# A gated three-mixer decoder block on one core: splits queued behind the gates' evictions, and another order inside the attention steps

## The chip, the cores and the metric

The kernel runs on one core of a Trainium2 chip. The metric is the device time of one execution in microseconds (us). The median of three runs of the kernel before is 353.12 us (352.27 to 354.44).

The core's engines each work through a queue of their own, in the order in which the program put the instructions there: TensorE (PE; its weight loads are shown as PEld), VectorE (DVE), ScalarE (ACT), GpSimd (POOL) and SyncE (SP), which issues the DMA transfers.

## What is computed

One decoder layer for 256 tokens of width 1024, in float32. The input is normed and multiplied by one wide weight matrix; from the product come queries, keys and values of three mixers, a gate for each mixer, and merge logits. The core of the reference:

```python
h = rmsnorm(x, norm_w[l])
proj = h @ w_in[l]
pieces = jnp.split(proj, IN_SPLIT_POINTS, axis=-1)
...
o_a = dilated_mixture(groups, slopes_a).reshape(B, S, D_A)
o_b = moba_attention(heads(b_q), heads(b_k), heads(b_v), slopes_b).reshape(B, S, D_B)
kv = rmsnorm(mem, mem_norm_w[l]) @ w_mem_kv[l]
m_k, m_v = jnp.split(kv, 2, axis=-1)
o_m = memory_cross_attention(heads(m_q), heads(m_k), heads(m_v)).reshape(B, S, D_M)
p_a = (o_a * jax.nn.silu(a_gate)) @ w_branch_a[l]
p_b = (o_b * jax.nn.silu(b_gate)) @ w_branch_b[l]
p_m = (o_m * jax.nn.silu(m_gate)) @ w_branch_m[l]
g_a, g_b, g_m = jnp.split(jax.nn.sigmoid(merge_logits + b_merge[l]), N_BRANCHES, axis=-1)
merged = g_a * p_a + g_b * p_b + g_m * p_m
x = x + merged @ w_out[l]
return rmsnorm(x, final_norm_w)
```

Mixer A has 8 heads in three dilation groups, mixer B 8 heads of causal attention, mixer M 4 heads over 256 memory tokens.

## The kernel before

**Chunks.** The weights are cut into 54 chunks (the list `PLAN`), nearly all of 1 MB. The main loop takes them in order: 0 to 5 are Bq, Bk and Bv, 6 to 10 the gates (b, b, a, a, m), 11 Mq, 12 Mk, 13 Mv, 14 to 31 mixer A, then merge logits and output products of the branches, and the last four the output projection. A full-precision product is made of three products in the faster format fp32r: the weights are split into a high part `wh` (ScalarE, line 93) and a low part `wl` (VectorE, line 94), and so are the activations (`hh`, `hl`). A chunk is two halves of 24 matmuls of 128x256: in each, 16 read `wh` (lines 232 and 233) and 8 read `wl` (line 235), in this order. There are three buffers for raw weights, three for `wh`, two for `wl`. So a part of chunk i can only be written when the chunk that held its buffer has been read.

**PSUM.** A chunk's result goes to one of three PSUM buffers (`pj`), which is free again when it has been evicted. The eviction of a gate is a tanh on ScalarE (line 645) and an operation of VectorE (line 647, tile `g`). Chunk 9 needs the buffer of chunk 6, chunk 10 that of chunk 7, and so on.

**Splits.** Queries and keys of mixer B are split too: `split_q` (lines 271 and 272) and `split_k` (283, 284 on ScalarE, 289, 290 on VectorE), for two halves of the heads (Bq0, Bk0, Bq1, Bk1). They are written out at chunks 6 to 11. The memory is normed by `mem_norm` (squares at line 171, then lines 143, 144, 175) and split by `mem_split` (line 218 on ScalarE, 219 on VectorE; tiles `mh`, `ml`), at chunks 9 to 11; chunk 12 reads them.

**Order.** On VectorE, ScalarE, GpSimd and SyncE a scheduler of the framework orders the instructions when the program is built: it places each by its own estimate of when the operands are ready, and so can place work well ahead of where it is written. `tc.issue_after(x)` keeps work behind instruction x. From chunk 8 on TensorE's order is as written.

**Attention steps.** The attention of each pair of heads is cut into steps, which `pump` slips between the halves of the chunks, two slots (one chunk) apart: for mixers B and M scores, transposes, products; for mixer A the first scores, transposes with the second scores, transposes, products. The steps of the next pair begin one chunk later (B, M) or two chunks later (A), so that several steps fall due in one slot. `chain` sorts them by slot and then by a second number: before, the later step of a pair goes first (`-j`). A step of scores needs two PSUM banks (pool `s`, two buffers), whose last readers are VectorE's minima (line 306), and a transpose needs rows that VectorE has scaled (line 314, tile `u`).

Of the kernel before, what the change touches and what calls it, by code (L numbers as in the profile page):

```python
# [1 line left out]

# [5 lines left out]
F32 = mybir.dt.float32  # L8
F32R = mybir.dt.float32r
BF16 = mybir.dt.bfloat16  # L10
AF = mybir.ActivationFunctionType
# [52 lines left out]
def kernel(ctx: ExitStack, tc: tile.TileContext, wts: bass.AP, xT_d: bass.AP, memT_d: bass.AP,  # L64
# [278 lines left out]
    def pair_steps_a(pair):  # L343
        hf, f = pair // 2, pair % 2
        us, pts, nbs = {}, {}, {}

        def view(n, g):
            return qkv["A" + n, hf, g].rearrange("p (f t) -> p f t", f=2)

        def scores(par):  # L350
            if par == 0:
                for s in range(2):
                    nbs[s] = tp.tile([P, 512], F32, tag="nb", name="nba")
                    nc.gpsimd.tensor_scalar(nbs[s], tab_a, SLOPES_A[2 * pair + s], 1.0, op0=ALU.mult, op1=ALU.mult)  # L354
            banks = [pa.tile([P, 512], F32, tag="s", name="sa") for _ in range(2)]
            for s in range(2):
                if par == 0:
                    out = banks[s].rearrange("p (a b) -> p a b", a=2)[:, :, 0:P]
                else:
                    out = banks[s][:, 0:S]  # L360
                score(out, qkv["Aq", hf, 0], qkv["Ak", hf, 0], s, f, slice(P * par, P * (par + 1)), slice(0, S))
            for g in range(1, 3):
                for s in range(2):
                    rows = slice(HD * s, HD * (s + 1))
                    for r in range(2):
                        ts = slice(P * par + 64 * r, P * par + 64 * (r + 1))
                        lo = P * (par + 1) + 64 * (g - 1)
                        nc.tensor.matmul(banks[s][64 * r:64 * (r + 1), lo:lo + 64], view("q", g)[rows, f, ts],
                                         view("k", g)[rows, f, ts], start=True, stop=True)
            for s in range(2):  # L370
                us[s, par] = tp.tile([P, 512], F32, tag="u", name="u", bufs=4)
                softmax(banks[s], nbs[s][:, P * (1 - par):P * (4 - par)], us[s, par], 0, 384)

        def trans(par):
            for s in range(2):
                if par == 0:
                    pts[s] = tp.tile([P, 3, 2, P], F32, tag="ptsb", name="ptsb", bufs=3)
                transposes(us[s, par], (0, 2, 1) if par == 0 else (0, 1, 2), pts[s][:, :, par, :])

        def pv():  # L380
            o = pa.tile([P, 512], F32, tag="o", name="oa", bufs=1)
            v0 = qkv["Av", hf, 0].rearrange("p (e c) -> p e c", e=2)
            vs = stacked[hf]
            for j in range(2):
                for s in range(2):
                    cols = slice(HD * (2 * f + s), HD * (2 * f + s + 1))
                    nc.tensor.matmul(o[HD * s:HD * (s + 1), 0:S], v0[:, j, cols],
                                     pts[s][:, j].rearrange("p e q -> p (e q)"), start=(j == 0), stop=False)
            for par in range(2):
                for r in range(2):  # L390
                    for s in range(2):
                        cols = slice(HD * (2 * f + s), HD * (2 * f + s + 1))
                        lo = P * par + 64 * r
                        nc.tensor.matmul(o[HD * s:HD * (s + 1), lo:lo + 64], vs[:, par, r, cols],
                                         pts[s][:, 2, par, 64 * r:64 * (r + 1)], start=False, stop=(par == 1 and r == 1))
            gated(o, "a", pair, False)

        return [lambda: scores(0), lambda: (trans(0), scores(1)), lambda: trans(1), pv]

    def pair_steps_b(pair):  # L400
        hf, f = pair // 2, pair % 2
# [68 lines left out]
    def chain(pairs, first, each):  # L470

        for n, fns in enumerate(pairs):
            for j, fn in enumerate(fns):
                steps.append((first + each * n + 2 * j, -j, fn))
        steps.sort(key=lambda z: z[:2])

    def out_mm(kc, wi, t):
# [46 lines left out]
                cs = slice(512 * (n // 2), 512 * (n // 2 + 1))  # L524
                nc.sync.dma_start(out[P * t:P * (t + 1), cs], yt[:, cs])

    late = []

    def evac_b(i, kind, key, ps, ps1):
        t = qkv[kind, key] = rtile(f"{kind}{key}")  # L530
# [15 lines left out]
    for i, (kind, key, src, col) in enumerate(PLAN):  # L546
# [15 lines left out]
        if i + 2 < NCH:  # L562
            for j in range(2 if i < 2 else 1):
                split(i + 2, j, 4 if i < 2 else 2)
        if i in (6, 8):
            hf = (i - 6) // 2
            qkv["Bqx", hf] = split_q(qkv["Bq", hf], 1.0, f"Bq{hf}")
        if i in (7, 11):
            hf = (i - 7) // 4
            qkv["Bkx", hf] = split_k(qkv["Bk", hf], f"Bk{hf}")  # L570
        if i == 9:
            mem_norm()
        if i in (10, 11):
            mem_split(4 * (i - 10), 4 * (i - 9))
        nat = kind[0] == "B"
        ah, al = (XH, XL) if nat else (HH, HL)
        if src == "mem":
# [64 lines left out]
                nc.scalar.mul(t, ps, -SCALE if kind == "Aq" else 1.0)  # L642
        elif kind == "G":
            th = tp.tile([P, 512], F32, tag="th", name="thg")
            nc.scalar.activation(th, ps, AF.Tanh, scale=0.5)
            g = gate[key] = rp.tile([P, 512], F32, tag="g", name=f"g{i}", bufs=5)
            nc.vector.scalar_tensor_tensor(g, th, 1.0, ps, op0=ALU.add, op1=ALU.mult)  # L647
        elif kind == "L":
            br, bk = key
            th = ths[br, bk] = tp.tile([P, 512], F32, tag="th", name="thl")  # L650
# [124 lines left out]
```

## Time and profile before

| | before |
|---|---|
| median of the runs | 353.12 us |
| profiled execution | 352.46 us |
| its span, first to last instruction | 350.6 us |
| TensorE busy | 337.4 us, 96% |
| VectorE busy | 232.5 us, 66% |
| ScalarE busy | 208.6 us, 60% |
| mean granted clock of TensorE | 0.989 |

The span is the time of the profiled execution without what lies around the program. Busy time says little on an engine that is always busy; what it waits for, and at which granted clock it works, is read from the views below. [...] All times in rows are microseconds from the start of the span, if not marked ns.

### The profile page before, as it was taken

How to read it: one execution, taken by the hardware profiler on the slowest of the kernel's cores; microseconds unless marked ns; L12 is line 12 of the kernel's file. 1: busy time of each engine (PE TensorE's matmuls, PEld its weight loads, DVE VectorE, ACT ScalarE, POOL GpSimd, SP SyncE). 2: the span in 40 equal slices, each digit the busy share in tenths (PEclk: the TensorE clock that was granted, in tenths of full speed). 3: DMA queues.
4: the chain of work that ended last, by engine and by line, in shares of the span. 5: the costliest groups of instructions: out<-in, count | busy, mean ns of one | idle time of the engine just before them, and what ended most of it. 6: DMA issues, size and time to landing. Idle time of an engine off the chain costs nothing.

```text
span 350.6 us, 7110 instructions
## 1 busy us (share of the span) xinstructions
PE 337.4 (96%) x2924; PEld 324.0 (92%) x2924; DVE 232.5 (66%) x402; ACT 208.6 (60%) x372; POOL 28.3 (8%) x40
## 2 busy tenths in 40 slices
PE   7999996999989999999999999999999999999992
PEld 4999995999989999899999999999999999999882
DVE  3859999658887457568756356866544748567554
ACT  6767899437776557766656365764643465546222
POOL 2501000000101000000101000010000214000022
PEclk9999998799999999999999999999999999999999
DMA  7997786646334463345333535444334366646003
GB/s 208 335 411 299 278 333 246 227 143 218 121 121 151 158 235 121 120 138 222 121 133 117 222 133 202 160 133 168 121 122 171 130 241 240 226 143 233 0 3 121
DMA packets 12945, 63.33 MB, mean 181 GB/s; under 512 B 1392, under 2 KB 2800, under 8 KB 6640
## 3 DMA queue, kind: packets, MB, share of 16 engines
q1 hardware_dynamic: 12912, 62.88, 49.9%
q8 instruction: 23, 0.38, 0.4%
q14 instruction: 10, 0.08, 0.1%
HBM read 61.82 MB, written 1.05 MB: 179 GB/s over the span
## 4 chain that ended last, share of the span: by engine, by line
PE 84%; DVE 6%; DMA 5%; ACT 2%; issue 1%; SPq 1%; POOL 0%; POOLq 0%; DVEq 0%
PE pj L232 16%; PE pj L235 16%; PE pj L233 16%; PE pj L252 4%; PE pj L254 4%; PE pj L253 4%; PE pt L320 3%; PE pw L232 3%; PE pw L233 3%; PE pw L235 3%; DMA wraw<-in_wts 3%; DMA xn<-in_x 2%; PE y L492 2%; PE y L491 2%; PE y L493 2%; DVE wl L94 2%
## 5 line engine op out<-in xcount | busy, mean ns | idle before, releaser
L94 DVE TENSOR_TENSOR wl<-wraw,wh 128x1024 fp32r<-128x1024 f32 (+2 forms) x117 | 129.4, 1143 | 60.1 <-issue 33.8
L93 ACT CAST wh<-wraw 128x1024 fp32r<-128x1024 f32 (+2 forms) x117 | 108.0, 968 | 49.9 <-PE pj L233 33.9
L232 PE MATMUL pj<-hh,wh 128*128 128x256 f32 x480 | 116.3, 284 | 3.4 <-DVE g L647 3.4
L233 PE MATMUL pj<-hl,wh 128*128 128x256 f32 x480 | 114.9, 280 | 0.2 <-DVE hl L199 0.2
L232 PEld LDWEIGHTS pj<-hh,wh 128*128 128x128 f32 x480 | 91.6, 191 | 4.5 <-issue 4.1
L233 PEld LDWEIGHTS pj<-hl,wh 128*128 128x128 f32 x480 | 91.6, 191 | 0.4 <-DVE hl L199 0.4
L235 PE MATMUL pj<-hh,wl 128*128 128x256 f32 x480 | 65.6, 280 | 0.0
L235 PEld LDWEIGHTS pj<-hh,wl 128*128 128x128 f32 x480 | 60.2, 190 | 0.0
L252 PE MATMUL pj<-wh,hh 128*128 128x256 f32 x96 | 26.9, 281 | 0.0
L254 PE MATMUL pj<-wh,hl 128*128 128x256 f32 x96 | 26.6, 277 | 0.0
L253 PE MATMUL pj<-wl,hh 128*128 128x256 f32 x96 | 26.6, 277 | 0.0
L321 ACT COPY ptsb<-pt 128x384 f32<-128x384 f32 (+1 forms) x28 | 13.2, 496 | 22.4 <-PE pt L320 22.4
L312 ACT ACTIVATE u<-u,st 128x384 f32<-128x384 f32 (+2 forms) x32 | 16.8, 527 | 10.2 <-DVE st L306 10.0
L252 PEld LDWEIGHTS pj<-wh,hh 128*128 128x128 f32 x96 | 18.0, 188 | 0.1
L253 PEld LDWEIGHTS pj<-wl,hh 128*128 128x128 f32 x96 | 18.0, 188 | 0.0
L254 PEld LDWEIGHTS pj<-wh,hl 128*128 128x128 f32 x96 | 18.0, 188 | 0.0
L314 DVE TENSOR_SCALAR u<-u,st 128x256 f32<-128x256 f32 (+2 forms) x40 | 15.5, 396 | 0.9
L354 POOL TENSOR_SCALAR nba<-con 128x512 f32<-128x512 f32 x8 | 5.0, 623 | 125.2 <-DVE st L306 124.8
L492 PE MATMUL y<-wl,mgh 128*128 128x512 f32 (+1 forms) x40 | 13.9, 348 | 0.0
L491 PE MATMUL y<-wh,mgh 128*128 128x512 f32 (+1 forms) x40 | 13.9, 347 | 0.0
L493 PE MATMUL y<-wh,mgl 128*128 128x512 f32 (+1 forms) x40 | 13.9, 346 | 0.0
L320 PE MATMUL pt<-con,u 128*128 128x128 f32 x88 | 12.5, 277 | 1.2 <-DVE u L314 1.2
(195 smaller groups left out, 549.2 us busy)
## 6 DMA issues: line engine op xcount, KB each, us to landing
wraw<-in_wts SPq DMA_DIRECT2D x48, 1024.0 KB, 4.8
wraw<-in_wts SPq DMA_DIRECT2D x15, 256.0 KB, 5.8
xn<-in_x SPq DMA_DIRECT2D x1, 1024.0 KB, 8.5
memT<-in_memT SPq DMA_DIRECT2D x1, 1024.0 KB, 5.6
memn<-in_mem SPq DMA_DIRECT2D x1, 1024.0 KB, 7.8
xres<-in_xr SPq DMA_DIRECT2D x1, 1024.0 KB, 6.0
wraw<-in_wts SPq DMA_DIRECT2D x2, 512.0 KB, 3.2
out<-ysb SPq DMA_DIRECT2D x4, 256.0 KB, 2.0
```

What stands on the lines that cost most here:

```text
L93: nc.scalar.copy(whs[i][:, sl], raws[i][:, sl])
L94: lower[i] = nc.vector.tensor_tensor(wls[i][:, sl], raws[i][:, sl], whs[i][:, sl].bitcast(F32), op=ALU.subtract)
L232: nc.tensor.matmul(ps[:, lo:lo + S], wh[:, k, fs], ah[k], start=(k == 0), stop=False)
L233: nc.tensor.matmul(ps[:, lo:lo + S], wh[:, k, fs], al[k], start=False, stop=False)
L235: nc.tensor.matmul(ps[:, lo:lo + S], wl[:, k, fs], ah[k], start=False, stop=(k == kn - 1))
L252: nc.tensor.matmul(ps[:, lo:lo + S], ah[k], wh[:, k, :], start=(k == 0), stop=False)
L253: nc.tensor.matmul(ps[:, lo:lo + S], ah[k], wl[:, k, :], start=False, stop=False)
L254: nc.tensor.matmul(ps[:, lo:lo + S], al[k], wh[:, k, :], start=False, stop=(k == KD - 1))
L320: nc.tensor.transpose(ps[:, P * j:P * (j + 1)], u[:, P * c:P * (c + 1)], ident)
L491: nc.tensor.matmul(y[t, n][:, 0:w], ht, wh[:, k, cs], start=(kc == 0 and k == 0), stop=False)
L492: nc.tensor.matmul(y[t, n][:, 0:w], ht, wl[:, k, cs], start=False, stop=False)
L493: nc.tensor.matmul(y[t, n][:, 0:w], lt, wh[:, k, cs], start=False, stop=(kc == 3 and k == 1))
```

## The change

Three things are changed; no instruction is added or taken away.

1. The splits of Bq, Bk and the memory are written at other chunks and put behind the two instructions of a gate's eviction (`behind_gate`): Bq0 and Bk0 behind gate 6, the memory's norm and split behind gate 8, Bq1 and Bk1 behind gate 9.
2. In `chain` the second number of the order changes: steps that fall due together now run as products, then scores, then transposes (mixer A: products, first scores, second scores, last transposes).
3. In mixer A the second scores are taken apart: the 64x64 scores at full precision (`far`) come first, then the transposes of the first half, then the other scores (`near`).

```diff
-        def scores(par):
+        def banks(par):
...
+        def near(ps, par):
...
+        def far(ps, par):
...
+        def weigh(ps, par):
             for s in range(2):
                 us[s, par] = tp.tile([P, 512], F32, tag="u", name="u", bufs=4)
-                softmax(banks[s], nbs[s][:, P * (1 - par):P * (4 - par)], us[s, par], 0, 384)
+                softmax(ps[s], nbs[s][:, P * (1 - par):P * (4 - par)], us[s, par], 0, 384)
+
+        def first():
+            ps = banks(0)
+            near(ps, 0)
+            far(ps, 0)
+            weigh(ps, 0)
+
+        def second():
+
+            ps = banks(1)
+            far(ps, 1)
+            trans(0)
+            near(ps, 1)
+            weigh(ps, 1)
...
-        return [lambda: scores(0), lambda: (trans(0), scores(1)), lambda: trans(1), pv]
+        return [first, second, lambda: trans(1), pv]
...
-                steps.append((first + each * n + 2 * j, -j, fn))
+                steps.append((first + each * n + 2 * j, (j + 1) % len(fns), fn))
...
-    late = []
+    late, gates = [], {}
+
+    @contextmanager
+    def behind_gate(i):
+
+        th, g = gates[i]
+        with tc.issue_after(th.ins), tc.issue_after(g.ins):
+            yield
...
-        if i in (6, 8):
-            hf = (i - 6) // 2
-            qkv["Bqx", hf] = split_q(qkv["Bq", hf], 1.0, f"Bq{hf}")
-        if i in (7, 11):
-            hf = (i - 7) // 4
-            qkv["Bkx", hf] = split_k(qkv["Bk", hf], f"Bk{hf}")
-        if i == 9:
-            mem_norm()
-        if i in (10, 11):
-            mem_split(4 * (i - 10), 4 * (i - 9))
+        if i in (7, 10):
+            hf = (i - 7) // 3
+            with behind_gate(i - 1):
+                qkv["Bqx", hf] = split_q(qkv["Bq", hf], 1.0, f"Bq{hf}")
+                if i == 7:
+                    qkv["Bkx", hf] = split_k(qkv["Bk", hf], f"Bk{hf}")
+        if i == 11:
+            with behind_gate(9):
+                qkv["Bkx", 1] = split_k(qkv["Bk", 1], "Bk1")
+        if i in (9, 10):
+            with behind_gate(8):
+                if i == 9:
+                    mem_norm()
+                mem_split(4 * (i - 9), 4 * (i - 8))
...
-            nc.scalar.activation(th, ps, AF.Tanh, scale=0.5)
+            a = nc.scalar.activation(th, ps, AF.Tanh, scale=0.5)
             g = gate[key] = rp.tile([P, 512], F32, tag="g", name=f"g{i}", bufs=5)
-            nc.vector.scalar_tensor_tensor(g, th, 1.0, ps, op0=ALU.add, op1=ALU.mult)
+            gates[i] = (a, nc.vector.scalar_tensor_tensor(g, th, 1.0, ps, op0=ALU.add, op1=ALU.mult))
```

Where the scheduler puts the work is seen in the order of the queues. The first place is VectorE's queue from the low part of chunk 8 (`wl8`) to the eviction of gate 6 (`g6`); before, it reads:

```order
L94 TENSOR_TENSOR wl8_576<-wraw8_501,wh8_575 128x1024 x2
L219 SCALAR_TENSOR_TENSOR ml_858<-memT_505,small_174,mh_857 128x256 x8
L94 TENSOR_TENSOR wl9_643<-wraw9_573,wh9_642 128x1024 x2
L272 SCALAR_TENSOR_TENSOR Bq1x0_721<-Bq1_565,Bq1x0_721 64x512
L272 SCALAR_TENSOR_TENSOR Bq1x1_724<-Bq1_565,Bq1x1_724 64x512
L289 TENSOR_TENSOR Bk1z0_934<-Bk1_429,Bk1y0_928 64x512
L290 TENSOR_TENSOR Bk1z0_934<-Bk1_429,Bk1y0_928 64x512
L647 SCALAR_TENSOR_TENSOR g6_638<-thg_636,pj6_585 128x512
```

And VectorE's queue from the same place in the changed kernel, up to the eviction of gate 7:

```order
L94 TENSOR_TENSOR wl8_576<-wraw8_501,wh8_575 128x1024 x2
L680 SCALAR_TENSOR_TENSOR g6_632<-thg_630,pj6_579 128x512
L272 SCALAR_TENSOR_TENSOR Bq0x0_640<-Bq0_562,Bq0x0_640 64x512
L272 SCALAR_TENSOR_TENSOR Bq0x1_643<-Bq0_562,Bq0x1_643 64x512
L289 TENSOR_TENSOR Bk0z0_652<-Bk0_427,Bk0y0_646 64x512
L290 TENSOR_TENSOR Bk0z0_652<-Bk0_427,Bk0y0_646 64x512
L94 TENSOR_TENSOR wl9_637<-wraw9_573,wh9_636 128x1024
L289 TENSOR_TENSOR Bk0z1_655<-Bk0_427,Bk0y1_649 64x512
L290 TENSOR_TENSOR Bk0z1_655<-Bk0_427,Bk0y1_649 64x512
L94 TENSOR_TENSOR wl9_637<-wraw9_573,wh9_636 128x1024
L680 SCALAR_TENSOR_TENSOR g7_711<-thg_709,pj7_658 128x512
```

The gate's eviction now follows `wl8` at once; the memory's splits (`ml`) and those of Bq1 and Bk1 have left this stretch, and those of Bq0 and Bk0, which stood ahead of `wl8`, are now behind the gate.

The second place is VectorE's queue in the softmax of mixer B's pair 0 (its rows are `u_1052` for one head and `u_1065` for the other) and the split of chunk 14, around the end of chunk 12. Before:

```order
L313 RECIPROCAL st_1053<-st_1053 128x1
L313 RECIPROCAL st_1058<-st_1058 128x1
L314 TENSOR_SCALAR u_1052<-u_1052,st_1053 128x256
L313 RECIPROCAL st_1066<-st_1066 128x1
L314 TENSOR_SCALAR u_1052<-u_1052,st_1058 128x128
L313 RECIPROCAL st_1071<-st_1071 128x1
L314 TENSOR_SCALAR u_1065<-u_1065,st_1066 128x256
L314 TENSOR_SCALAR u_1065<-u_1065,st_1071 128x128
L94 TENSOR_TENSOR wl14_1012<-wraw14_922,wh14_1011 128x1024 x2
L622 TENSOR_TENSOR Mk_1102<-pj12_1015,rb_m_975 128x512
```

The same stretch of VectorE's queue in the changed kernel, where `u_1159` and `sb_1147` belong to pair 1:

```order
L313 RECIPROCAL st_1058<-st_1058 128x1
L314 TENSOR_SCALAR u_1052<-u_1052,st_1053 128x256
L314 TENSOR_SCALAR u_1052<-u_1052,st_1058 128x128
L313 RECIPROCAL st_1066<-st_1066 128x1
L94 TENSOR_TENSOR wl14_1012<-wraw14_930,wh14_1011 128x1024 x2
L655 TENSOR_TENSOR Mk_1102<-pj12_1015,rb_m_975 128x512
L313 RECIPROCAL st_1071<-st_1071 128x1
L314 TENSOR_SCALAR u_1065<-u_1065,st_1066 128x256
L306 ISA u_1159,st_1160<-sb_1147,nbb_1157 128x256
L306 ISA st_1160 128x1
L314 TENSOR_SCALAR u_1065<-u_1065,st_1071 128x128
```

The last two scalings of pair 0 have moved behind the low part of chunk 14, the eviction of Mk and a minimum of pair 1.

The third place is TensorE's queue in the middle of chunk 13, where pair 0's transposes (`pt`, of the rows named above) and pair 1's scores (`sb`) fall due together. Before:

```order
L320 MATMUL pt_1148<-con_106,u_1052 128x128 x3
L320 MATMUL pt_1154<-con_106,u_1065 128x128 x3
L296 MATMUL sb_1159<-Bk0y0_646,Bq0x0_579 128x256
L297 MATMUL sb_1159<-Bk0z0_652,Bq0x0_579 128x256
L296 MATMUL sb_1160<-Bk0y1_649,Bq0x1_582 128x256
L297 MATMUL sb_1160<-Bk0z1_655,Bq0x1_582 128x256
L296 MATMUL sb_1159<-Bk0y0_646,Bq0x0_579 128x128
L297 MATMUL sb_1159<-Bk0z0_652,Bq0x0_579 128x128
L296 MATMUL sb_1160<-Bk0y1_649,Bq0x1_582 128x128
L297 MATMUL sb_1160<-Bk0z1_655,Bq0x1_582 128x128
```

TensorE's queue there in the changed kernel:

```order
L296 MATMUL sb_1147<-Bk0y0_646,Bq0x0_640 128x256
L297 MATMUL sb_1147<-Bk0z0_652,Bq0x0_640 128x256
L296 MATMUL sb_1148<-Bk0y1_649,Bq0x1_643 128x256
L297 MATMUL sb_1148<-Bk0z1_655,Bq0x1_643 128x256
L296 MATMUL sb_1147<-Bk0y0_646,Bq0x0_640 128x128
L297 MATMUL sb_1147<-Bk0z0_652,Bq0x0_640 128x128
L296 MATMUL sb_1148<-Bk0y1_649,Bq0x1_643 128x128
L297 MATMUL sb_1148<-Bk0z1_655,Bq0x1_643 128x128
L320 MATMUL pt_1184<-con_106,u_1052 128x128 x3
L320 MATMUL pt_1190<-con_106,u_1065 128x128 x3
```

The scores have moved ahead of the transposes. On SyncE one transfer moves: the load of the residual stands one weight load later.

## Rows read from the trace of the kernel before

**Rows 1.** The page: busy time by engine, and TensorE's granted clock in 40 slices.
```profile
PE 337.4 (96%) x2924; PEld 324.0 (92%) x2924; DVE 232.5 (66%) x402; ACT 208.6 (60%) x372; POOL 28.3 (8%) x40
...
PEclk9999998799999999999999999999999999999999
```

**Rows 2.** Waits of TensorE: engine, line, waited for, us in total, times, longest.
```profile
PE pj L232 <- DVE g L647: 3.4, 1, 3.4
PE pt L320 <- DVE u L314: 1.2, 2, 1.0
```

**Rows 3.** Table by stage: stretch, its length, busy time by engine, granted clock.
```profile
56.97:60.51 3.54, 0.16 (x3) 0.03 (x1) 3.44 (x6) 3.54 (x7) 0.00 (x0) 0.83 0.70 250
60.51:66.15 5.64, 5.64 (x26) 5.64 (x27) 5.28 (x9) 2.83 (x4) 0.71 (x1) 0.50 0.64 230
68.84:74.28 5.44, 5.44 (x50) 5.44 (x50) 2.96 (x3) 2.49 (x4) 0.00 (x0) 1.00 0.37 120
80.18:86.58 6.40, 6.40 (x58) 6.40 (x58) 5.97 (x19) 4.73 (x13) 0.81 (x2) 1.00 0.58 196
```

**Rows 4.** Timeline of TensorE: start, length, instruction, count, idle before and its end.
```profile
46.20 1.07 PE L235 MATMUL pj<-hh,wl 128*128 128x256 f32 x8
...
60.51 0.55 PE L232 MATMUL pj<-hh,wh 128*128 128x256 f32 x1 [3.38 <-DVE g L647]
...
89.13 0.82 PE L320 MATMUL pt<-con,u 128*128 128x128 f32 x6
...
98.23 0.98 PE L320 MATMUL pt<-con,u 128*128 128x128 f32 x6 [1.00 <-DVE u L314]
```

**Rows 5.** Timeline of VectorE, chunks 8 and 9, then chunk 12's end.
```profile
49.03 2.36 DVE L94 TENSOR_TENSOR wl<-wraw,wh 128x1024 fp32r<-128x1024 f32 x2
51.30 3.25 DVE L219 SCALAR_TENSOR_TENSOR ml<-memT,small,mh 128x256 fp32r<-128x256 f32 x8
54.47 2.36 DVE L94 TENSOR_TENSOR wl<-wraw,wh 128x1024 fp32r<-128x1024 f32 x2
56.86 1.39 DVE L272 SCALAR_TENSOR_TENSOR Bq1x<-Bq,Bq1x 64x512 fp32r<-64x512 f32 x2
...
59.67 0.69 DVE L647 SCALAR_TENSOR_TENSOR g<-thg,pj 128x512 f32<-128x512 f32 x1
...
83.59 0.42 DVE L306 CUSTOM_DVE_ANT_0 u<-sb,nbb 128x256 f32<-128x256 f32 x1 [0.30 <-PE sb L297]
...
85.55 0.22 DVE L313 RECIPROCAL st<-st 128x1 f32<-128x1 f32 x2
...
86.79 2.36 DVE L94 TENSOR_TENSOR wl<-wraw,wh 128x1024 fp32r<-128x1024 f32 x2
```

**Rows 6.** Timeline of ScalarE, chunks 7 to 9, then mixer M's second pair.
```profile
46.80 3.31 ACT L218 ACTIVATE mh<-memT,small 128x256 fp32r<-128x256 f32 x8
...
54.50 0.60 ACT L645 ACTIVATE thg<-pj 128x512 f32<-128x512 f32 x1
...
56.40 1.06 ACT L171 ACTIVATE memn<-memn 128x1024 f32<-128x1024 f32 x1
...
58.97 3.87 ACT L93 CAST wh<-wraw 128x1024 fp32r<-128x1024 f32 x4
...
141.92 0.47 ACT L312 ACTIVATE u<-sm,st 128x256 f32<-128x256 f32 x1
```

**Rows 7.** DMA issues from 44 to 45.5: count, size, us to landing.
```profile
wraw<-in_wts SPq DMA_DIRECT2D x1, 1024.0 KB, 8.0
```

**Rows 8.** Timeline of GpSimd: the inverse root of the memory's squares.
```profile
62.07 0.71 POOL L144 TENSOR_TENSOR ssq_m<-ssq_m,half 128x2 f32<-128x2 f32 x1 [33.64 <-DVE ssq_m L143]
```

**Rows 9.** The chain that ended last, in order of time: start, length, what.
```profile
164.70 0.94 PE pj L235 x8
...
168.47 0.66 PE pt L320 x6
...
184.40 0.80 PE pt L320 x6
```

More of the change, by code (lines that the diff above doesn't have):

```diff
@@ L1 @@
-from contextlib import ExitStack
+from contextlib import ExitStack, contextmanager
 import concourse.bass as bass
@@ L354, in scores @@
                     nc.gpsimd.tensor_scalar(nbs[s], tab_a, SLOPES_A[2 * pair + s], 1.0, op0=ALU.mult, op1=ALU.mult)
-            banks = [pa.tile([P, 512], F32, tag="s", name="sa") for _ in range(2)]
+            return [pa.tile([P, 512], F32, tag="s", name="sa") for _ in range(2)]
+        def near(ps, par):
             for s in range(2):
                 if par == 0:
-                    out = banks[s].rearrange("p (a b) -> p a b", a=2)[:, :, 0:P]
+                    out = ps[s].rearrange("p (a b) -> p a b", a=2)[:, :, 0:P]
                 else:
-                    out = banks[s][:, 0:S]
+                    out = ps[s][:, 0:S]
                 score(out, qkv["Aq", hf, 0], qkv["Ak", hf, 0], s, f, slice(P * par, P * (par + 1)), slice(0, S))
+        def far(ps, par):
             for g in range(1, 3):
@@ L367, in scores @@
                         lo = P * (par + 1) + 64 * (g - 1)
-                        nc.tensor.matmul(banks[s][64 * r:64 * (r + 1), lo:lo + 64], view("q", g)[rows, f, ts],
+                        nc.tensor.matmul(ps[s][64 * r:64 * (r + 1), lo:lo + 64], view("q", g)[rows, f, ts],
                                          view("k", g)[rows, f, ts], start=True, stop=True)
+        def weigh(ps, par):
             for s in range(2):
                 us[s, par] = tp.tile([P, 512], F32, tag="u", name="u", bufs=4)
-                softmax(banks[s], nbs[s][:, P * (1 - par):P * (4 - par)], us[s, par], 0, 384)
+                softmax(ps[s], nbs[s][:, P * (1 - par):P * (4 - par)], us[s, par], 0, 384)
[10 more added lines that the diff above has]
+            weigh(ps, 1)
         def trans(par):
```

## The prediction

> **What bounds the kernel now.** Read the page first: TensorE is busy 96% of the span of 350.6 us, the other engines 66% or less [rows 1]. Nothing that this change does shortens TensorE's work, since every instruction is kept; only its idle time, its clock and its pitch can move. So the second view is the list of what TensorE waits for: one wait of 3.4 us for a line-647 result of VectorE (a gate's eviction), and two, 1.0 us at the longest, for softmax rows that a transpose needs [rows 2]. Third, the table by stage shows what the long wait costs. Chunk 8 ends at 56.97, chunk 9 starts at 60.51 and ends at 68.84: 11.87 us, where chunk 10 takes 5.44 [rows 3]. [...]
>
> Why it waits is read on VectorE and ScalarE. Chunk 9 needs a PSUM buffer, the pool has three, and chunk 6 holds the one that is due. Chunk 6's last matmuls start at 46.2, so it is complete at 47.1 [rows 4]. Yet its gate leaves VectorE only at 60.36, behind eight memory splits (from 51.30), chunk 9's low part, and Bq1's and Bk1's splits [rows 5]. ScalarE is as late: the memory's casts start at 46.80, before any gate's tanh [rows 6].
>
> **Step 1, gates before splits.** In the new order g6 stands right behind wl8, and the tanh of gate 6 behind wh9. wh9 may start when chunk 6's high parts are read, 46.2. Two casts of 0.97 and a tanh of 0.6 [rows 6] give 48.8, or later by as much as wh9's load lands after 46.2. wl8 can only start at chunk 6's end, 47.1, and takes 2.3: 49.4; then the gate, 0.69 [rows 5]: 50.1. Chunk 9 asks at 56.97, so 6.8 us are to spare. Walking on in the same way, with Bq0's and Bk0's splits (four of 0.7, then two) and wl9 between, g7 is done at 57.3 (asked for at 62.4), g8 at 60.2 (67.9), g9 at 67.8 (73.8), g10 at 74.9 (80.2). wl9 ends at 56.6 and is first read 1.8 us into chunk 9. Chunk 10's weights took 8.0 us to land from 44.81 [rows 7], 52.8, and are cast from 53.5. The stage becomes 5.44: **-6.43 us**. Bounds: -3.54 if the clock falls all the same, -6.5 at most.
>
> **Step 2, the moved splits.** What was moved has to stand somewhere. ScalarE finishes wh11 at 58.1, gate 8's tanh at 58.6 and both squares of the memory at 60.8 [rows 6]. From there VectorE has no pause that I can find. GpSimd's 0.71 [rows 8] lets the diagonal end at 62.4; then, from 62.8: wl11 2.27, five memory splits 1.98, g9 0.69, Bq1 1.39, wl12 2.27, Bk1 2.8, g10 0.69, wl13 2.27, Mq 0.70, four score minima with Mq's other half 1.96, and the first scalings 0.74 of the 1.24 that all of pair 0 take (all by [rows 5]; the 64x512 splits are 0.70 each); the sum is 17.8, so 80.6. Here the new order puts wl14 and Mk ahead of the last two scalings of pair 0, where before they followed them. wl14 can't start before chunk 12's end, 86.58 - 6.43 = 80.15 [rows 3]. 80.6 + 2.27 + 0.69 + 0.35 (reciprocal, scaling) + 0.35 (a minimum of pair 1) + 0.20 = 84.5. TensorE reaches chunk 13's middle at 89.13 - 6.43 = 82.70 [rows 4], now does pair 1's scores first (0.96: 6.40 less 5.44 in the stage of chunk 12 [rows 3]) and one triple of transposes (0.29), and stands at 83.95 before the second triple: a new wait of **+0.5 us**. Without wl14 ahead the rows would have been ready by 82. Bounds: +0.2, since wl14's floor of 80.15 alone gives 84.1; and +1.6, if each of a dozen hand-offs on that chain costs 0.1 more, as the 0.12 between wl9 (54.47 + 2.27) and Bq1 (56.86) does [rows 5]. The other things that were moved are covered: the memory's splits end at 67.1 and chunk 12 asks at 73.75; wl12 and wl13 end 2 us ahead; the residual's load goes out one weight load later and is read only at the end.
>
> **Step 3, scores before transposes.** The wait of 1.0 us stands before pair 1's transposes in chunk 14 [rows 2, 4]. Now pair 2's scores, 0.96, go first, and their banks are free once pair 1's minima are read (85.0). By the walk pair 1's last scaling is done at 91.3 and its transposes begin at 92: **-1.1 us** (bounds 0 and -1.3). The other wait, 0.2 before a transpose of mixer m [rows 2], hung on an exponential that ScalarE did at 141.92, after two casts of weights [rows 6]; it now stands ahead of them: **-0.3** (0 to -0.4; by starts of matmuls it costs 0.36). For pairs 2 and 3 the order only adds 0.96 us before transposes that did not wait; copies of transposed rows come as much later, and their products a whole chunk of 5.4 us later.
>
> **Step 4, mixer A.** Six steps swap 64x64 scores, transposes and 128-row scores. Six transposes take 0.66 behind ordinary matmuls and 0.80 behind products of 64 columns [rows 9]: a change of shape costs about 0.14. In the two steps with products the 64x64 scores now follow them, and 128-row scores lead back into the chunk, one change fewer: **-0.3** for both (0 to -0.5). In the rest the count is the same. A last thing is not explained by any row: eight matmuls take 0.91 in some half chunks (5.44 for 48 [rows 3]) and 0.94 in others [rows 9]. The state changes at such steps or between chunks; all slow halves together cost about 2.9 us (some 570 matmuls by 5 ns). Each step keeps the same set of instructions, so I take 0, and +-1 for the range.
>
> **Sum.** -6.43 + 0.5 - 1.1 - 0.3 - 0.3 = -7.6 us. The profiled execution took 352.46 us with a span of 350.65, the median of the runs is 353.12, 0.66 above it. So 344.8 by the profiled execution and 345.5 by the median; I take 345.2.
>
> **Rivals.** *The backlog takes more of it back.* VectorE runs without a pause for 22 us; were its hand-offs at the upper bound, pair 0's transposes would wait 1.6 instead of 0.5, and pair 1's perhaps 0.6: 345.2 + 1.7 = 346.9. For it: the dense stretch is where the kernel's slack is now spent. Against: the list was made with the trace's own durations.
>
> *The clock falls anyway.* A wait that is left, in chunk 9 or at 84, could bring the clock to 0.50 as the long one did, for about 5.6 us: +2.8, so 348.0. Against it stands the wait of 1.0 us at 98: the slices of the clock show 9 there [rows 1]. [...]
>
> *The gate is not what holds chunk 9.* If something else were as late (wl9, or the landing of a load), the idle time would shrink little: with 3 of the 3.54 us left and the clock down, 345.2 + 5.9 = 351, about no change. The walk leaves wl9 2 us.
>
> *Slower.* The memory's splits, done by 54.5 before, now end at 67.1; chunk 12 reads all of them from 73.75. If gates, squares and loads pushed them by a further 6.6 us, TensorE would stand idle there. It decides from about 11.5 us of delay: 4.9 of idle and 2.8 of clock eat the whole gain; 15 us give 345.2 + 8.4 + 2.8 = 356.4. Nothing on the list is that long.
>
> **Chances.** Forecast 0.63 (own range 343.4 to 346.4), backlog 0.18, clock 0.08, other holder 0.07, slower 0.04. Runs of one kernel spread over 2 us, so 1% (3.5 us) is what can be told from no change. Under 349.6 lie the first three: faster 0.89; the fourth is the same, 0.07; slower 0.04. The range reaches from 343.2 (pitch and shape changes at their best) to 348.4 (the clock's case), and leaves out the last two and the edges.
>
> **What would show it.** Right: TensorE's waits hold no row for a gate (line 680), the stage of chunk 9 takes 5.44 at a clock of 1.00, gate 6 ends near 50 on VectorE, and the longest wait left is a transpose at about 84 for a scaling that stands behind wl14. Step 3 is right if no wait is left at chunk 14 (now near 92). Wrong: a wait of chunk 9 for weights, a clock slice of 8 or less near 57 or 84, or a wait at 84 over 1.6 us. A span below 341.5 would mean that the pitch moved, which I count at nothing.

## The result and the profile after

The changed kernel takes 348.53 us (median of six runs, 348.16 to 349.71) against 352.69 us before (six runs beside them, 351.84 to 354.44): a ratio of 0.988, with a 95% interval of 0.985 to 0.991. The direction was forecast, the size was not: -7.6 us were expected and -4.2 came, so that the time lies 3.3 us above the forecast and 0.13 above the upper end of its range. The profiled execution took 348.68 us with a span of 346.9 (352.46 and 350.65 before), so the spans differ by 3.7 us: 4.0 up to the last matmul, less 0.3 behind it.

The page of the changed kernel, busy time by engine and TensorE's granted clock; it answers [rows 1]:

```profile
PE 336.8 (97%) x2924; PEld 323.7 (93%) x2924; DVE 233.3 (67%) x402; ACT 208.1 (60%) x372; POOL 27.2 (8%) x40
...
PEclk9999999999999999999999999999999999999997
```

TensorE's list of waits (engine, line, waited for, us in total, times, longest), for [rows 2]. The gate's row is gone, and of the transposes' one wait is left:

```profile
PE pt L320 <- DVE u L314: 1.5, 1, 1.5
```

The table by stage, chunks 9 and 10, for [rows 3]. Chunk 9, which took 11.87 us with its wait, takes 5.44 at a clock of 1.00:

```profile
57.19:62.63 5.44, 5.44 (x50) 5.44 (x49) 3.85 (x7) 5.14 (x9) 0.29 (x1) 1.00 0.73 261
62.63:68.07 5.44, 5.44 (x50) 5.44 (x49) 5.44 (x12) 5.44 (x11) 0.43 (x1) 1.00 0.96 339
```

VectorE's timeline (start, length, instruction, count), for [rows 5]. Gates 6 and 7 end at 50.55 and 57.87; the walk of step 1 had 50.1 and 57.3. Further down wl14 and Mk stand ahead of pair 0's last two scalings, as step 2 said:

```profile
49.87 0.68 DVE L680 SCALAR_TENSOR_TENSOR g<-thg,pj 128x512 f32<-128x512 f32 x1
...
57.19 0.68 DVE L680 SCALAR_TENSOR_TENSOR g<-thg,pj 128x512 f32<-128x512 f32 x1
...
81.97 2.34 DVE L94 TENSOR_TENSOR wl<-wraw,wh 128x1024 fp32r<-128x1024 f32 x2
84.34 0.69 DVE L655 TENSOR_TENSOR Mk<-pj,rb_m 128x512 f32<-128x512 f32 x1
...
85.02 0.33 DVE L314 TENSOR_SCALAR u<-u,st 128x256 f32<-128x256 f32 x1
...
85.61 0.28 DVE L314 TENSOR_SCALAR u<-u,st 128x128 f32<-128x128 f32 x1
```

TensorE's timeline at the same place, for [rows 4]: the second three transposes wait 1.47 us, where +0.5 was forecast.

```profile
83.96 0.51 PE L320 MATMUL pt<-con,u 128*128 128x128 f32 x3
85.95 0.55 PE L320 MATMUL pt<-con,u 128*128 128x128 f32 x3 [1.47 <-DVE u L314]
```

ScalarE's timeline, for [rows 6], shows where that second came from. The cast of chunk 11's weights starts at 57.49 and not at the walk's 56.1, because it waits for their load; gate 8's tanh and the memory's squares stand behind it:

```profile
57.49 2.00 ACT L93 CAST wh<-wraw 128x1024 fp32r<-128x1024 f32 x2 [2.12 <-DMA wraw<-in_wts]
59.40 0.59 ACT L678 ACTIVATE thg<-pj 128x512 f32<-128x512 f32 x1
59.88 1.05 ACT L171 ACTIVATE memn<-memn 128x1024 f32<-128x1024 f32 x1
```

What the wait lists don't show is read from the start times of matmuls. The table cuts the program at the first (or last) matmul into a named tile and gives the time between the cuts, in us, for this kernel and for runs told below. The tiles `sb`, `sm` and `sa` are the scores of mixers B, M and A, `oa` the products of mixer A, `y` the output; branch b is mixer B.

| stretch | before | after | gates_only | order_only | key_only | second_only | wl14_late | wl14_t1 |
|---|---|---|---|---|---|---|---|---|
| chunk 3's middle to chunk 11's | 52.15 | 45.88 | 45.91 | 50.10 | 45.91 | 45.90 | 45.87 | 47.07 |
| then to the first sb | 5.90 | 5.90 | 5.90 | 5.88 | 5.90 | 5.90 | 5.90 | 5.88 |
| branch b: to the first sm | 44.50 | 45.24 | 45.65 | 43.76 | 44.98 | 44.69 | 43.97 | 43.76 |
| mixer M: to the first sa | 34.35 | 34.02 | 34.35 | 34.02 | 34.02 | 34.35 | 34.02 | 34.02 |
| mixer A: to the last oa | 97.75 | 96.91 | 97.75 | 96.91 | 97.50 | 96.84 | 96.91 | 96.95 |
| tail: to the first y | 62.83 | 65.27 | 62.83 | 65.27 | 65.27 | 62.83 | 65.27 | 62.83 |
| output projection | 22.04 | 22.04 | 22.04 | 22.04 | 22.04 | 22.04 | 22.04 | 22.04 |

The tail has no attention step and no wait in either kernel, the same 552 matmuls of 128x256, a clock of 1.00, and yet takes 2.44 us more: its matmuls start every 0.1178 us instead of every 0.1133 (this time from start to start is called the pitch). Twenty us of the tail before hold 179 matmuls (the first count), and the same stretch of the changed kernel, shown further down, holds 172:

```profile
262.00:282.00 20.00, 20.00 (x179) 20.00 (x178) 11.55 (x12) 8.99 (x14) 3.50 (x2) 1.00 0.44 145
```

That is the larger half of the miss. Most stretches repeat within 0.05 us wherever the same instructions stand in the same order, so in mixers M and A and in the tail the effects of the two halves of the change can be added up. In branch b they can't: the new order gives 0.74 us there alone (`order_only` against before), and 0.41 beside the moved splits (after against `gates_only`).

### The profile page after: what moved, and what is told of

Read it like the earlier page. It is cut to its first block, busy times and chain, and to the rows that moved or that the text cites. A ratio compares the mean times of both kernels' runs of the same rounds, so it can differ in the third digit from the quotient of the medians.

```text
span 346.9 us, 7107 instructions
## 1 busy us (share of the span) xinstructions
PE 336.8 (97%) x2924; PEld 323.7 (93%) x2924; DVE 233.3 (67%) x402; ACT 208.1 (60%) x372; POOL 27.2 (8%) x40
## 3 DMA queue, kind: packets, MB, share of 16 engines
HBM read 61.82 MB, written 1.05 MB: 181 GB/s over the span
## 4 chain that ended last, share of the span: by engine, by line
PE 86%; DVE 4%; DMA 4%; SPq 2%; ACT 2%; issue 1%; POOL 0%; POOLq 0%; DVEq 0%
PE pj L232 16%; PE pj L235 16%; PE pj L233 16%; PE pj L252 5%; PE pj L254 4%; PE pj L253 4%; PE pt L320 3%; PE pw L232 3%; PE pw L233 3%; PE pw L235 3%; DMA xn<-in_x 2%; PE y L513 2%; PE y L514 2%; PE y L515 2%; DVE wl L94 2%; DMA wraw<-in_wts 1%
## 5 line engine op out<-in xcount | busy, mean ns | idle before, releaser
L232 PE MATMUL pj<-hh,wh 128*128 128x256 f32 x480 | 114.9, 281 | 0.0
L232 PEld LDWEIGHTS pj<-hh,wh 128*128 128x128 f32 x480 | 90.4, 188 | 0.7 <-issue 0.6
L233 PEld LDWEIGHTS pj<-hl,wh 128*128 128x128 f32 x480 | 90.4, 188 | 0.4 <-DVE hl L199 0.4
```

Source lines behind the costliest of these rows:

```text
L232: nc.tensor.matmul(ps[:, lo:lo + S], wh[:, k, fs], ah[k], start=(k == 0), stop=False)
L233: nc.tensor.matmul(ps[:, lo:lo + S], wh[:, k, fs], al[k], start=False, stop=False)
```

## Experiments

Two theories were tested. **A:** the missing second at 84 comes from the late landing of chunk 11's weights; rival: VectorE's list is too long by itself. **B:** the order of mixer steps sets the pitch of the matmuls behind them; rival: the pitch moved with the gates, or with timing.

### The two halves of the change alone

`gates_only` keeps the order of steps and the inner order of mixer A's second step as before:

```
-  steps.append((first + each * n + 2 * j, (j + 1) % len(fns), fn))
+  steps.append((first + each * n + 2 * j, -j, fn))
...
-  far(ps, 1)
   trans(0)
   near(ps, 1)
+  far(ps, 1)
```

> The changed kernel with only its first half: splits stand behind the gates, but mixer steps run in the old order (transposes, then scores; in mixer A transposes, 128-row scores, 64x64 scores). My account: the wait of chunk 9 and its slow clock are gone (-6.43), transposes of pair 0 are asked for 0.96 us earlier than in the changed kernel while their rows are ready at the same time, so they wait 2.4 (not 1.47), and chunk 14's transposes wait about 1 us as before; the tail from 256 us on runs at the 0.113 us pitch, since the old order of steps leads into it: span 350.6 - 6.4 + 2.4 = 346.6. Rival, that moving the gates is what changed the pitch of the tail: tail at 0.118, span 349.1. Rival, that the new order is what brought the wait at 84: no wait there, span 344.2.

Measured: 348.08 us (ratio 0.988, 0.984 to 0.992), span 346.1. Its list of waits, and from its table by stage 20 us of the tail (the first count is that of the matmuls):

```profile
PE pt L320 <- DVE u L314: 2.2, 2, 2.0
```
```profile
260.00:280.00 20.00, 20.00 (x179) 20.00 (x178) 10.17 (x12) 9.35 (x14) 3.50 (x2) 1.00 0.58 192
```

The same 20 us of the changed kernel:

```profile
260.00:280.00 20.00, 20.00 (x172) 20.00 (x172) 9.51 (x10) 9.34 (x14) 3.50 (x2) 1.00 0.56 203
```

The first half alone gives all that the whole change gives. Transposes that ask 0.88 us earlier (by their starts) wait 2.0 us, not 2.4, since VectorE had their rows 0.39 us earlier too, and the tail keeps the 0.113 us pitch. One expectation failed: chunk 14's wait of about 1 us is gone here as well, though the steps stand in the old order (the second wait of the list, 0.2 us, is mixer M's).

`order_only` puts the splits back where they stood before (chunks 6 to 11, without `behind_gate`) and keeps the new order.

> The changed kernel with only its second half: mixer steps in the new order, splits where they stood before. My account: chunk 9 waits 3.4 us for its gate and runs at half clock as before; the waits of chunk 14 (1.1) and of mixer M (0.36) are gone, mixer A's steps with products are 0.2 shorter; but the tail from about 260 us on runs at the 0.118 us pitch (+2.5): span 350.6 - 1.7 + 2.5 = 351.4. Rival, that the pitch does not hang on the order of steps: tail at 0.113, span 348.9.

Measured: 353.11 us (ratio 1.0006, 0.998 to 1.003), span 349.4. The second half alone gains nothing that can be measured: its tail is at 0.118 us, +2.44, while branch b gives -0.74, mixer M -0.33 and mixer A -0.84. The span came out 2 us below expectation, in a profiled execution (351.22 us) that is the fastest of the ten; the median is about what the expected span would give. The wait of chunk 9 is there, and the table by stage of the wait and of the chunk behind it reads:

```profile
57.36:60.89 3.53, 0.16 (x2) 0.03 (x1) 3.42 (x6) 3.53 (x7) 0.00 (x0) 1.00 0.76 251
60.89:66.33 5.44, 5.44 (x46) 5.44 (x47) 5.29 (x9) 3.23 (x5) 0.71 (x1) 1.00 0.72 238
```

Behind the same wait, to 0.02 us, the clock stood at 1.00 here and at 0.50 for 5.64 us in the profile of before [rows 3]; no run shows what makes the difference. In the timed runs of the kernel before the mean clock over the whole program goes from 0.988 to 0.997, in those of the changed kernel, which has no such wait, from 0.994 to 0.997. So the clock's share of step 1, the 2.89 us that chunk 9 took over chunk 10's 5.44 once it had started (60.51 to 68.84) [rows 3], was a price of the profiled execution; by these means, which show no single stretch, some runs paid little or nothing of it. Behind its wait `order_only` ran chunks 9 to 11 at the slower pitch (0.118 us), 120 matmuls more than before, which took 0.5 us back.

### Which reordering moves the tail's pitch

`key_only` has the new order between pairs and the old second step of mixer A; `second_only` the reverse (each is one of the two edits shown above).

> The changed kernel with mixer A's second step in the old order (transposes, 128-row scores, 64x64 scores); the order between pairs stays new. If the inner order of that step is what leads the tail into the slow pitch: tail at 0.113 us from 256 on, span 346.9 - 2.5 + 0.2 = 344.6. If the order between pairs does it: tail at 0.118, span 347.1.

> The changed kernel with the old order between pairs (transposes before scores) and mixer A's second step in the new order. If the order between pairs leads the tail into the slow pitch: tail at 0.113, wait at 84 about 2 us and at chunk 14 up to 1 us as with the old order, span 346.9 - 2.5 + 1.5 = 345.9. If the inner order does it: tail at 0.118, span 348.4.

Measured, one profile each: 350.56 us with a span of 348.8, and 347.70 with 345.9. The table by stage for the same 20 us, `key_only` first:

```profile
260.00:280.00 20.00, 20.00 (x172) 20.00 (x172) 10.50 (x12) 9.34 (x14) 3.50 (x2) 1.00 0.50 184
```
```profile
260.00:280.00 20.00, 20.00 (x179) 20.00 (x178) 9.99 (x11) 9.34 (x14) 3.51 (x2) 1.00 0.57 193
```

With the new order between pairs the tail ran at 0.118 us (`key_only`), with the new inner order of the second step alone at 0.113 (`second_only`); the inner order gives 0.91 us in mixer A (97.75 to 96.84). `key_only`'s span is 1.7 us above expectation mainly because it waited 1.8 us for its first weights at the start, which put everything 1.5 us later. That `second_only` met its 345.9 is chance: it too started 1.7 us later, but the wait at 84 was 1.0 and not 2, and none stood at chunk 14.

### The wait at 84

`memn_late` fetches the memory's rows behind chunk 11's weights:

```
+  if i == 8:
+      with tc.issue_after(fetched[11].ins):
+          mem_load_rows()
```

(`fetched[11]` is the load of chunk 11's weights; `mem_load_rows` issues the load of `memn`, which `mem_load` did before.)

> The changed kernel with one load moved: the memory's rows (1 MB) are fetched behind chunk 11's weights, not ahead of chunk 10's. My account of the wait at 84 (1.47 us, forecast 0.5): chunk 11's weights landed late beside that load, so ScalarE's cast, the squares and VectorE's whole list came 1.3 us later. Then the weights land by 55.4, the squares begin near 58.0, and the wait at 84 shrinks to 0.2 to 0.5: span 346.9 - 1.1 = 345.8 at an unchanged pitch. Rival, that VectorE's list itself is too long (its hand-offs, and wl14 that can't start before chunk 12's end): the wait stays at 1.3 or more, span 346.7.

Measured: 348.98 us (ratio 0.990, 0.987 to 0.993), span 347.6, not faster. The load of chunk 11's weights took 4.8 us instead of 7.4, the cast no longer waited for it but for TensorE's last use of the buffer, and the wait at 84 shrank to 0.26. ScalarE, then TensorE:

```profile
57.76 2.01 ACT L93 CAST wh<-wraw 128x1024 fp32r<-128x1024 f32 x2 [1.52 <-PE pj L235]
```
```profile
86.58 0.55 PE L322 MATMUL pt<-con,u 128*128 128x128 f32 x3 [0.26 <-DVE u L316]
```

The test is not clean: from chunk 6's middle to chunk 11's the matmuls ran at 0.118 us here (46.93 for the first stretch of the table, +1.05), which makes TensorE ask later, so that most of the fall comes from that, and eats the gain. But other profiles of kernels with the same order up to that place decide it, since the load lands early or late in them by itself. Six of them, by what the cast of chunk 11 waited for, and the wait at 84: the load, 1.47 (after), 1.23 (`t1_t2`), 1.21 (`key_only`), 0.60 (`dup1`); TensorE, 0.48 (`pokes`) and 0.47 (`t1_dup`). The cast starts between 13.30 us (after) and 14.31 us (`pokes`) ahead of chunk 11's middle, and in all six this lead and the wait add up to 14.8 us. One of each, `dup1` and then `pokes`:

```profile
57.23 2.00 ACT L93 CAST wh<-wraw 128x1024 fp32r<-128x1024 f32 x2 [1.25 <-DMA wraw<-in_wts]
...
85.69 0.55 PE L322 MATMUL pt<-con,u 128*128 128x128 f32 x3 [0.60 <-DVE u L316]
```
```profile
57.37 2.01 ACT L93 CAST wh<-wraw 128x1024 fp32r<-128x1024 f32 x2 [1.12 <-PE pj L233]
...
85.84 0.55 PE L320 MATMUL pt<-con,u 128*128 128x128 f32 x3 [0.48 <-DVE u L314]
```

Theory A holds: with the load in time the wait is the 0.5 us of the forecast, and every bit that the load is late comes on top.

`wl14_late` takes the other cause away, wl14's place ahead of the scalings:

```
+  if i == 12:
+      with tc.issue_after(scaled[0].ins):
+          split(14, 0, 2)
+          split(14, 1, 2)
```

(`scaled[0]` is pair 0's last scaling.)

> The changed kernel with VectorE's low part of chunk 14's weights queued behind the last scaling of branch b's pair 0 (in the changed kernel it stands ahead of it). My account of the wait at 84: the 2.3 us of wl14 ahead of the last two scalings are all of it; the scalings then end at 83.3, TensorE asks at 84.5, the wait is gone: span 346.9 - 1.5 = 345.4 at an unchanged pitch. Rival, that the delay only moves on: pair 1's minima and scalings come later, and the wait stands at chunk 14's transposes (near 93) with 0.5 us or more: span 346 or above.

Measured: 347.90 us (ratio 0.988, 0.985 to 0.990), span 345.3. VectorE and TensorE:

```profile
81.92 0.53 DVE L314 TENSOR_SCALAR u<-u,st 128x256 f32<-128x256 f32 x2
82.36 2.36 DVE L94 TENSOR_TENSOR wl<-wraw,wh 128x1024 fp32r<-128x1024 f32 x2
```
```profile
83.62 0.84 PE L320 MATMUL pt<-con,u 128*128 128x128 f32 x6
...
92.01 0.98 PE L320 MATMUL pt<-con,u 128*128 128x128 f32 x6
```

The six transposes at 84 run without a wait. Branch b takes 43.97 us against 45.24, so 1.27 of the 1.48 us are gained. A part of the delay has moved on to chunk 14, as the rival had it, in small, where the list of waits doesn't show it: by the starts TensorE stands 0.27 us longer before the six transposes at 92.01 than in the changed kernel, and 0.10 longer before the fourth of them (they take 0.98 us, 0.84 in the changed kernel).

### What a step does to the pitch

`dup1` does the first matmul of chunk 38 twice:

```
+  for _ in range(1 if k == 0 and (wi, lo) == (38, 0) else 0):
+      nc.tensor.matmul(ps[:, lo:lo + S], wh[:, k, fs], ah[k], start=True, stop=True)
```

> The changed kernel with one matmul more: the first matmul of chunk 38 (near 257 us) is done twice. [...] If the pitch is set by the shape of the steps ahead and then lasts, one more matmul costs 0.12: span 347.0, tail at 0.118.

Measured: span 346.7 (349.01 us; ratio 0.990, 0.987 to 0.993), tail at 0.118. One more matmul inside the stretch changed nothing behind it; some 500 matmuls at 0.113 us would have taken 2.2 us less.

`pokes` puts small products, whose results nothing reads, between half chunks of the tail (chunk, half: form and count; t is a transpose, r a product of 128 columns, s, v and f the full fp32 ones):

```
+  POKES = {(38, 0): "t6", (38, 1): "t6", (39, 0): "t1", (39, 1): "t1", (40, 0): "t2", (41, 0): "t2", (41, 1): "t3",
+           (42, 0): "t3", (42, 1): "t4", (43, 0): "t4", (44, 0): "r1", (44, 1): "r1", (45, 0): "r2", (45, 1): "r2",
+           (46, 0): "s1", (47, 0): "s2", (47, 1): "v1", (48, 0): "v2", (48, 1): "f1", (49, 0): "f2"}
```

> The changed kernel with small extra products, whose results nothing reads, put between the half chunks of the tail (chunks 38 to 49), where no step of a mixer stands and the pitch otherwise never changes: 6, 6, 1, 1, 2, 2, 3, 3, 4, 4 transposes of 128x128, then products of 128 columns (1, 1, 2, 2), of 64x64 (1, 2), of 64 stationary columns by 256 (1, 2), and full fp32 products of 256 columns (1, 2). If a step flips the pitch by what it issues, some of these flip the 24 to 96 matmuls behind them between 0.118 and 0.113 us and the same group does it twice: the six transposes above all, since a lone set of six flipped the pitch at 186 and at 246 us in the changed kernel and at 192 and 252 in the one before. If the pitch hangs on something else (how long a step takes, what other engines or loads do then), none or no regular pattern.

Measured, span 354.3: the pitch did change there, with no attention step and no softmax. But the sets of six transposes kept it both times, against the expectation. Of transposes and products of 128 columns, odd numbers changed it six times in six, even ones kept it seven times in eight, the sixes included: that looked like a parity. `t1_t2` tests it with one transpose at each of ten places and two at each of the ten behind them:

> The changed kernel with one extra transpose at each of ten places of the tail (chunks 38 to 43), then two at each of ten more (chunks 44 to 49). If an odd number flips the pitch and an even number keeps it: ten changes in turn, 0.113, 0.118, 0.113 and so on, back to 0.118 after the tenth, then no change over the ten pairs. If the state depends on more than the count: an irregular pattern in both.

Measured (span 349.6): no parity, but a pattern. Behind single transposes the half chunks went 0.113, 0.118, 0.118, 0.118 and again so; behind pairs 0.113, 0.113, 0.118. The chain that ended last (start, length, what), where eight matmuls take 0.91 or 0.94 us; first behind single transposes, then behind pairs:

```profile
258.41 0.91 PE pj L235 x8
...
261.32 0.94 PE pj L235 x8
...
264.26 0.94 PE pj L235 x8
...
267.20 0.94 PE pj L235 x8
```
```profile
287.68 0.91 PE pj L235 x8
...
290.66 0.91 PE pj L235 x8
...
293.67 0.94 PE pj L235 x8
...
296.68 0.91 PE pj L235 x8
```

`gates_t1` puts one transpose ahead of chunk 37 into `gates_only`.

> The kernel with the gates' half alone (old order of steps, tail at 0.113 us) with the same one transpose ahead of chunk 37. If an odd number flips the pitch whichever it is: tail at 0.118, span 346.1 + 2.5 = 348.6. If a transpose there always leads into the fast pitch: tail at 0.113, span 346.2.

Measured: span 346.8. The half chunk behind the transpose went to 0.118, but mixer A's last products, which follow it, led back to 0.113 for the whole tail. So neither account held: the tail is where the second one had it, but not because the transpose led there.

`t1_dup` has single transposes at all twenty places and repeats the matmul behind each, once in the first ten, three times in the last ten.

> As the run with extra transposes, but one transpose at all twenty places, and behind each the first matmul of the half chunk done twice in the first ten, four times in the last ten. There, half chunks with one transpose ahead went fast, slow, slow, slow, fast (a pattern of four), those with two fast, fast, slow (of three). If the state hangs on how many products have gone by (25 to a half chunk with one transpose, 26 with two), the first ten now have 26 and go in a pattern of three, like those with two transposes. If it hangs on the small products alone, the first ten keep the pattern of four. If on time gone by, one more matmul of 0.113 us shifts the pattern to another that is regular too.

Measured (span 352.8): 0.113 and 0.118 in turn for the first ten, 0.113, 0.118, 0.118, 0.118 for the last. Neither the count of small products (that would leave the pattern of four) nor the count of all products (26 would give the pattern of three, as with pairs) explains it. What the runs show is that the pitch changed at such places, and that the pattern differed both with the products there (one transpose or two ahead of 24 matmuls: a pattern of four or of three) and with the number of matmuls between two such places (24, 25 or 27 behind one transpose: a pattern of four, of two, of four). No run shows the cause.

Attention steps are not the only places. The chunks of values (Bv, Av, Mv; lines 252 to 254) use weights and activations in exchanged places, with the same 128x256 products. Where such a chunk gives way to an ordinary one, with no other product between, the pitch changed in 98 of 112 cases in the fourteen profiles (8 of 8 before, 7 of 8 after); where it begins, in none of 112. The changed kernel's chain around such a place, with the last eight matmuls of the half chunk ahead of the values and of the one behind them:

```profile
206.56 0.91 PE pj L235 x8
...
212.68 0.11 PE pj L253
...
212.91 0.12 PE pj L232
...
214.79 0.94 PE pj L235 x8
```

### The version that beats both

`wl14_t1` is `wl14_late` with one transpose ahead of chunk 37, whose result nothing reads:

```
+  POKES = {(37, 0): "t1"}
```

> The changed kernel with chunk 14's low part behind the scalings of pair 0 (as the run before showed it) and one transpose of 128x128, whose result nothing reads, ahead of chunk 37. If an odd number of products of 128 columns flips the pitch (so it did six times in six in the run with the extra products), the tail from chunk 37 on runs at 0.113 us: 528 matmuls x 4.5 ns = -2.4, +0.1 for the transpose, span 345.3 - 2.3 = 343.0 and a median near 345.2. If that was chance, the tail stays at 0.118: span 345.4.

Measured: 346.37 us (ratio 0.981, 0.978 to 0.984), span 344.8, 2.2 us less than the changed kernel. The tail is at 62.83 again, for the wrong reason: after `gates_t1` this transpose is a lucky setting and no rule. Its table by stage:

```profile
260.00:280.00 20.00, 20.00 (x179) 20.00 (x179) 9.52 (x10) 9.39 (x15) 3.50 (x2) 1.00 0.61 212
```

The span is 1.8 us above expectation: 1.2 lie in the first stretch, which runs at 0.118 us throughout in this profile (47.07), and 0.9 are a later start.

## Why the prediction was right and where it failed

The sum, term by term, from the table of stretches (before against after, `order_only` where it isolates a term); mixer A's shapes from the starts of matmuls at its six changed steps, from the last one ahead of a step to the second one behind it:

| term | forecast | measured | from |
|---|---|---|---|
| chunk 9's wait and clock | -6.43 | -6.27 | 45.88 - 52.15 |
| new wait at 84 | +0.5 | +1.48 | 45.24 - 43.76 |
| chunk 14's wait | -1.1 | -0.74 | 43.76 - 44.50 |
| mixer M | -0.3 | -0.33 | 34.02 - 34.35 |
| mixer A, changes of shape | -0.3 | -0.61 | six steps, 14.97 to 14.36 |
| mixer A, pitch of its half chunks | 0 | -0.23 | the rest of -0.84 |
| tail, pitch | 0 | +2.44 | 65.27 - 62.83 |
| start of the program | 0 | +0.22 | chunk 3's middle, 24.69 to 24.91 |
| sum | -7.6 | -4.04 | to the last matmul |

**Step 1 held**, in its mechanism and, against the profiled execution, in its size: no gate wait, clock 1.00, gates 6 and 7 within 0.6 us of the walk. Its share for the clock was taken for a constant and isn't one, as `order_only` showed (1.00 behind the same wait).

**Step 2 had the right place and the right instructions, and was mis-sized: +1.48 for +0.5.** The failing line is "ScalarE finishes wh11 at 58.1". The walk looked up the landing of chunk 10's weights, 8.0 us [rows 7], and let chunk 11's be in time. It took 7.4 us, issued at 49.98 while the memory's rows and chunk 10's weights were still in flight (they landed 7.9 us after 42.76 and 8.1 us after 45.03):

```profile
wraw<-in_wts SPq DMA_DIRECT2D x1, 1024.0 KB, 7.4
```

In the kernel before the same load, issued at 51.45, took 4.7 us, and the casts of chunk 11 stood behind others. The upper bound of 1.6, made from hand-offs, held the value for a reason that wasn't the true one. The rival "the backlog takes more of it back" therefore came half true: its first wait is there (1.6 forecast, 1.47 found), its second (0.6 at chunk 14) isn't.

**Step 3 held where it stands alone**: in `order_only` there is no wait at chunk 14 and none in mixer M. Branch b gained 0.74 instead of 1.1, since 187 of its matmuls ran at the slower pitch and not 104 (+0.37). In the whole change its share at chunk 14 can't be told from that of step 1: the three profiles with the gates moved and the old order between pairs (`gates_only`, `second_only`, `gates_t1`) have no such wait either. There TensorE has waited 1.0 to 2.0 us at 84 and so comes later to chunk 14, which the prediction didn't reckon with.

**Step 4's shapes had the right sign and half the measured size, and its pitch failed.** The two steps with products gained 0.41 us (forecast 0.3), the other four 0.20 (forecast 0, since "the count is the same"). A good part lies behind the step, where the second matmul followed the first after 0.22 us, and now after 0.11 us in the four steps that end with 128-row scores. The first matmul's piece of the chain at a step with products, before and then after:

```profile
186.06 0.31 PE pj L232
```
```profile
180.32 0.11 PE pj L232
```

"Each step keeps the same set of instructions, so I take 0, and +-1 for the range" is the step that cost most: +2.44 in the tail, -0.23 in mixer A, and smaller shares in branch b. The prediction had seen both pitches, that they change at mixer steps or between chunks, and the sum of all 0.118 halves (2.9 us; a count by starts gives 575 x 4.4 ns = 2.6). What it missed is that the tail's pitch went with the order of the steps (0.118 us in `order_only`, 0.113 in `gates_only`), and that behind the last step lie 552 matmuls through which it stayed. One change of the pitch there is worth 552 x 4.4 ns = 2.4 us, far outside +-1. The right bound was in the trace: the longest stretch without a step or a chunk of values, times the difference. 345.2 + 2.4, with step 2's upper bound (+1.1), makes 348.7, which holds the result. The upper end of the stated range, 348.4, is put down to the clock's case, which the text itself works out as 348.0.

The other rivals: the clock didn't fall in the wait at 84 (1.00 from 83.96 to 86.25), the gate was what held chunk 9, and chunk 12 never waited for the memory's splits.

## What to carry to other kernels

A state that shows in the trace but has no known cause is not worth nothing: bound it by the longest stretch over which it can last. When work is moved ahead of a load, look up the landing of every load that the new order reads, not of the first alone. And take apart a change with two halves: here the first gives the whole gain, and the second gives 1.9 us in its own stretches when it is alone, 1.6 beside the first, and loses 2.4 in one that it doesn't touch.

## What the runs showed of the hardware

- Matmuls of 128x256 in fp32r, each with its own weights, ran at 0.1133 us from start to start (the tail before) or at 0.1178 (the tail after), both at a granted clock of 1.00; through the 552 matmuls of the tail the pitch stayed the same. At a granted clock of 0.50 they started every 0.213 us (before, 60.86 to 63.63 us). A full fp32 product of this size (line 181, tile `spread_x`) and the fp32r matmul behind it took 0.55 us together (before, 24.69 to 25.24); two fp32r matmuls take 0.23.
- The pitch changed at three kinds of places: where products of another shape stood between (after, from 0.1133 to 0.1178 at the six transposes at 245.13 us), at the end of a chunk of values (98 of 112 cases), and behind waits (`order_only` went from 0.113 to 0.118 us at its wait of 3.38 us). From mixer M's first scores to the first y, after, `order_only` and `wl14_late` take the same times (34.02, 96.91 and 65.27 us in the table of stretches), though the spans of after and `wl14_late` lie 1.6 us apart and `order_only` has the wait of 3.4 us ahead. In mixer M and the tail `key_only`, with the new order between pairs alone, takes them too (34.02 and 65.27); before and `gates_only` share others (34.35, 97.75 and 62.83). In the first stretch of the table, profiles with the splits behind the gates took 45.88 us (after), 46.93 (`memn_late`) and 47.07 (`wl14_t1`).
- Behind a wait of 3.38 us of TensorE its clock stood at 0.50 for 5.64 us in one profile (before), and at 1.00 in another (`order_only`).
